# Seven block products for the attention's output product, with sums of its weights made in the first layer

## The chip, the cores and the metric

The kernel runs on one core of a Trainium2 chip. The metric is the time of one execution in microseconds (us), as the device reports it; a kernel's time is the median of several runs. In the profile PE is TensorE, DVE VectorE, ACT ScalarE, POOL GpSimd and SP SyncE, which sends all the DMAs here.

## The reference

Two layers on 1024 tokens of width 1024, all in float32. The first is a retention layer with a gated output product; the second is latent attention with eight heads of width 128. What the change touches is the end of the second layer:

```python
def mla_layer(x, g_pre, w_in, g_q_lat, w_uq, w_out, g_post, k_nope, k_rope, v):
    ...
    o = mla_attention(q_nope, q_rope, k_nope, k_rope, v)
    y = (jax.nn.silu(gate) * o) @ w_out
    return x + rmsnorm(y, g_post)
```

`w_out` is 1024 x 1024 there. The first layer ends in the same way, with a `w_out` of 2048 x 1024.

## The kernel before

Each float32 operand is kept as two parts, hi and lo, and each product of two blocks is three matmuls: hi x lo, lo x hi, hi x hi (`mm3`, L229, its matmuls on L232 to L234). `split` (L236) makes the parts: a copy on ACT (L238) and a subtraction on DVE (L239). Nearly all data lies in a heap of 51 blocks of [128, 1024] (`Heap`, L33), which are used again in the order in which they come free, so a load can wait for an old block's last reader. A framework puts the instructions of each engine into their final order, from the order of the code and its own estimate of the times; what stands in a queue is done in that order.

The program has these stages: the retention layer; its output product `out_a` (L921); norm, residual and transposes of each 128 token tile, `post_a` (L995); the latents; the gates (`gates`, L1146); the attention (`attention`, L1258). `later(n, fn)` (L259) runs a piece of work n calls of `tick` later, so beside a later product. `out_a` already works with seven block products: halves of the tokens, of the 2048 rows and of the columns. A block product has four steps b of 24 matmuls of 128x512 (`tok_product`, L822), over four PSUM banks, and two ticks for each step. Loads of `yl` (left) and `wl` (right, the sums of weights from the DRAM tiles `td`) run ahead of them. Behind the last products come the tiles' `post_a`: an ACT square, a POOL power, two DVE operations, a second square, a scaled copy `hn`, and by `later(2, transpose)` eight TensorE transposes (L1019), whose banks ACT copies into the operands of the next stage.

In the attention the scores of head h, their softmax and the products with the values go block by block (`score`, `finish`, `values`), and the projections of head h+1 are dealt out among them as filler, by a share of columns. S tiles take two banks each, two of them; `acc` and `r` have two banks each. In the last head the filler is the output product (`out_units`, L1415): for each block of 256 tokens, from the last to the first, the gated outputs `gT` are split in eight pieces of 128x256, and each half of each token tile is one bank with 24 matmuls over all eight row blocks of `w_out`:

```python
            ps = self.bank("acc")
            yield from self.project(ps, u, lambda h: [w[:, ns] for w in self.wo[h]], NH)
            nc.scalar.activation(junk[:, ns], ps, AF.Square, accum_out=ss[:, n:n + 1])
            ...
            nc.vector.tensor_mul(y[:, ns], ps, self.gpost[:, ns])
```

Then the power on POOL (L256), a DVE operation per half for scale and residual (L1448), and the stores (L1450).

Of the kernel before, what the change touches and what calls it, by code (L numbers as in the profile page):

```python
# [18 lines left out]
P = 128  # L19
# [6 lines left out]
NH = 8  # L26
# [171 lines left out]
class Trunk:  # L198
# [26 lines left out]
    def bank(self, tag, shape=(P, HALF)):  # L225
        self.n += 1
        return self.ps.tile(list(shape), F32, tag=tag, name=f"{tag}_{self.n}")
# [48 lines left out]
    def weight_order(self):  # L276

        I = self.I
        for h in range(NH):
            if h % 2 == 0:  # L280
                yield I["w_pair"][h // 2], 896
            yield I["w_head"][h], 640
        for k in range(NH):
            yield I["w_out_b"][k * P:(k + 1) * P, :], DM
# [35 lines left out]
    def run(self):  # L320
        nc, tc, ctx, I = self.nc, self.tc, self.ctx, self.I
        self.sp = ctx.enter_context(tc.tile_pool(name="sp", bufs=1))
        self.heap = Heap(ctx.enter_context(tc.tile_pool(name="mp", bufs=1)), BLOCKS)
        dp = ctx.enter_context(tc.tile_pool(name="dp", bufs=1, space=DRAM))
        self.h1 = dp.tile([NT, P, DM], F32, name="h1")
        self.td = [[dp.tile([P, DM], F32, name=f"td{n}_{b}") for b in range(4)] for n in range(4)]
        self.vd = [[dp.tile([P, DM], F32, name=f"vd{h}_{half}") for half in range(2)] for h in range(NH)]
        self.yd = [[dp.tile([P, DM], F32, name=f"yd{h}_{half}") for half in range(2)] for h in range(NH)]
        self.gd = [dp.tile([P, DM], F32, name=f"gd{h}") for h in range(NH)]
# [11 lines left out]
        with tc.tile_pool(name="psA", bufs=4, space=PSUM) as self.ps:  # L341
            self.layer_a()
            self.out_a()
            self.latents()
            self.gates()
        with tc.tile_pool(name="psB", bufs=2, space=PSUM) as self.ps:
            self.attention()
# [573 lines left out]
    def out_a(self):  # L921
# [42 lines left out]
        self.X = {}  # L964
# [3 lines left out]
        self.later(9, lambda: self.operands(("A21", "A22")))  # L968
# [5 lines left out]

        fill(0, 4)
# [14 lines left out]

    def operands(self, names):
        for n in names:
            self.operand(n, self.A[n])

    def post_a(self, g, y, gpost):  # L995

        nc, I, heap = self.nc, self.I, self.heap
        x = heap.get("xres")
        nc.sync.dma_start(x, I["x"][g * P:(g + 1) * P, :])
# [28 lines left out]
        self.later(2, transpose)  # L1028
# [117 lines left out]
    def gates(self):  # L1146
# [3 lines left out]
        away = NH - 2  # L1150
        self.gT, left = [None] * NH, [4] * NH

        def sink(p):
            def take(i, j, bank, U):
                h = 2 * p + j
                if self.gT[h] is None:
                    self.gT[h] = heap.get("gT")
                c = self.gT[h][:, i * HALF:(i + 1) * HALF]
# [5 lines left out]
                left[h] -= 2  # L1164
                if not left[h] and h < away:
                    nc.sync.dma_start(self.gd[h], self.gT[h])
                    heap.free(self.gT[h])

            return take

        def back(h):
            self.gT[h] = heap.get("gT")
            nc.sync.dma_start(self.gT[h], self.gd[h])

        for p in range(NH // 2):
            if p == NH // 2 - 1:
                for n in (2, 3):
                    self.later(n, lambda n=n: self.prefetch(n - 1))
                for h in range(away):
                    self.later(4 + h, lambda h=h: back(h))  # L1180
# [9 lines left out]
    def head_projections(self, h):  # L1190
# [4 lines left out]
        def bank():  # L1195
# [3 lines left out]
            return self.bank("S", (P, 2, HALF))[:, 0, :] if h == 0 and n % 2 else self.bank("acc")  # L1199
# [58 lines left out]
    def attention(self):  # L1258
# [15 lines left out]
        for h in range(NH):  # L1274
# [4 lines left out]
            else:  # L1279
# [3 lines left out]
                share = (own + 24 * HALF * 4) / 8  # L1283
            for step in range(8):
# [15 lines left out]
                if h == NH - 1 and 1 <= step < 5:  # L1300
                    for _ in range(2):
                        self.prefetch(1)
                        self.wo.append(self.loaded.popleft())
            if h + 1 < NH:
                for _ in fill:
                    pass
        while open_tiles:
            self.finish(open_tiles.popleft())
        self.finish(None)
# [73 lines left out]
    def values(self, h, b, pT, blocks):  # L1383
# [8 lines left out]
        u = self.gT[h][:, b * 256:(b + 1) * 256]  # L1392
# [7 lines left out]
    def prepare_out(self):  # L1400
        heap = self.heap
# [5 lines left out]
        self.out_ready = set()  # L1407
        self.gpost = heap.get("gpostb")
        self.nc.sync.dma_start(self.gpost, self.I["g_post_b"])
        self.wo = []  # L1410
        self.lead = 2
        while len(self.fetched) < 2:
            self.fetch()

    def out_units(self):  # L1415

        nc, heap = self.nc, self.heap
        for b in range(NT // 2 - 1, -1, -1):
            blocks = [[heap.get("u", F32R) for _ in range(2)] for _ in range(2)]
            part = lambda x, h: x[h // 4][:, (h % 4) * 256:(h % 4) * 256 + 256]  # L1420
            for h in range(NH):
                while h == NH - 1 and b not in self.out_ready:
                    yield 0
                self.split(part(blocks[0], h), part(blocks[1], h), self.gT[h][:, b * 256:(b + 1) * 256])
            for i in (1, 0):
                yield from self.out_tile(2 * b + i, lambda h: [part(x, h)[:, i * P:(i + 1) * P] for x in blocks])
            heap.free(*blocks[0], *blocks[1])

    def out_tile(self, t, u):
# [3 lines left out]
        y, res, junk = heap.get("yb"), heap.get("hres"), heap.get("junkb")  # L1433
        nc.sync.dma_start(res, self.h1[t])
        for n in range(2):
            ns = slice(n * HALF, (n + 1) * HALF)
            ps = self.bank("acc")
            yield from self.project(ps, u, lambda h: [w[:, ns] for w in self.wo[h]], NH)
            nc.scalar.activation(junk[:, ns], ps, AF.Square, accum_out=ss[:, n:n + 1])
# [4 lines left out]
            nc.vector.tensor_mul(y[:, ns], ps, self.gpost[:, ns])  # L1444
        heap.free(junk)
        for n in range(2):
            ns = slice(n * HALF, (n + 1) * HALF)
            nc.vector.scalar_tensor_tensor(out=y[:, ns], in0=y[:, ns], scalar=r, in1=res[:, ns],  # L1448
                                           op0=ALU.mult, op1=ALU.add)
            nc.sync.dma_start(self.out[c, ns], y[:, ns])  # L1450
        heap.free(y, res)

# [31 lines left out]
def _layout(a):  # L1484
# [37 lines left out]
    L["w_out_b"] = A["w_out_b"][0]  # L1522
# [23 lines left out]
```

## Time and profile before

| | us |
|---|---|
| median of 3 runs | 1267.18 (1267.08 to 1267.78) |
| profiled execution | 1268.73 |
| its span | 1267.0 |
| PE busy | 1240.5 (98%) |
| DVE busy | 996.6 (79%) |
| ACT busy | 639.6 (50%) |

The granted clock is 0.999 of full speed over the span. The profile shows one execution; the busy time of PE holds matmuls that overlap at their ends, so a stage is read by TensorE's gaps and by the spacing of its work, and not by the sum of durations.

### The profile page before, as it was taken

What the parts mean: (1) busy time and instruction counts of PE and PEld (TensorE: products, weight loads), DVE (VectorE), ACT (ScalarE), POOL (GpSimd) and SP (SyncE); (2) the same over time, 40 slices, a digit from 0 to 9 for tenths busy, and PEclk for the clock granted to TensorE, in tenths of its full rate; (3) what the DMA queues carried; (4) which work ended last, traced back from release to release, by engine and by line L of the source; (5) the groups of instructions that cost most, each with busy time, mean ns of one, the idle gap of its engine ahead of it and who ended that gap; (6) DMA issues with size and microseconds to landing.
All of it is one profiled execution on the core that took longest, in us unless ns stands there. A gap on an engine that the chain in (4) does not pass through costs nothing. (4 is left out here: it accounts for less than half of the span.)

```text
span 1267.0 us, 17676 instructions
## 1 busy us (share of the span) xinstructions
PE 1240.5 (98%) x6568; PEld 1066.5 (84%) x6568; DVE 996.6 (79%) x1839; ACT 639.6 (50%) x1162; POOL 65.5 (5%) x86
## 2 busy tenths in 40 slices
PE   6999999999999999999999999999999999999997
PEld 5888878888888888888888789978898989898886
DVE  6888878898998998999966874675688788989622
ACT  7632125555564565565634875574445455456411
POOL 2000000000000000001000131200000000000000
PEclk9999999999999999999999999999999999999999
DMA  8248981232222322248663631124301020122321
GB/s 349 84 154 319 325 318 50 73 112 70 86 67 85 120 67 69 84 137 338 209 245 99 234 141 34 40 96 163 118 19 51 11 57 14 34 78 100 117 84 50
DMA packets 54166, 155.32 MB, mean 123 GB/s; under 512 B 6464, under 2 KB 15680, under 8 KB 54080
## 3 DMA queue, kind: packets, MB, share of 16 engines
q1 hardware_dynamic: 54080, 154.20, 34.9%
q8 instruction: 51, 0.84, 0.3%
q14 instruction: 35, 0.29, 0.1%
HBM read 113.28 MB, written 36.70 MB: 118 GB/s over the span
## 5 line engine op out<-in xcount | busy, mean ns | idle before, releaser
L232 PE MATMUL acc<-xhi,unit 128*128 128x512 f32 x560 | 220.6, 394 | 1.4 <-DVE unit L239 1.2
L233 PE MATMUL acc<-xlo,unit 128*128 128x512 f32 x560 | 219.2, 392 | 0.8 <-DVE xlo L239 0.8
L234 PE MATMUL acc<-xhi,unit 128*128 128x512 f32 x560 | 218.2, 390 | 0.0
L232 PEld LDWEIGHTS acc<-xhi,unit 128*128 128x128 f32 x560 | 105.3, 188 | 23.1 <-DVE unit L239 2.8
L234 PEld LDWEIGHTS acc<-xhi,unit 128*128 128x128 f32 x560 | 105.2, 188 | 21.7
L233 PEld LDWEIGHTS acc<-xlo,unit 128*128 128x128 f32 x560 | 105.4, 188 | 20.4 <-DVE xlo L239 1.1
L232 PE MATMUL acc<-vhi,xlo 128*128 128x512 f32 x224 | 89.3, 399 | 1.0 <-DVE xlo L239 1.0
L234 PE MATMUL acc<-vhi,xhi 128*128 128x512 f32 x224 | 88.4, 394 | 0.0
L233 PE MATMUL acc<-vlo,xhi 128*128 128x512 f32 x224 | 88.3, 394 | 0.0
L238 ACT ACTIVATE unit<-wsum 128x512 fp32r<-128x512 f32 x80 | 50.4, 631 | 59.9 <-PE acc L234 44.9
L1346 ACT ACTIVATE p<-S,nm 128x896 f32<-128x896 f32 (+3 forms) x64 | 47.4, 741 | 54.9 <-DVE nm L1343 50.2
L238 ACT ACTIVATE unit<-wraw 128x512 fp32r<-128x512 f32 x60 | 37.8, 630 | 53.6 <-issue 21.9
L238 ACT ACTIVATE pT<-r 128x512 fp32r<-128x512 f32 (+2 forms) x96 | 44.5, 489 | 37.8 <-PE r L1376 37.7
L238 ACT ACTIVATE vhi<-wv 128x1024 fp32r<-128x1024 f32 x28 | 29.3, 1060 | 64.4 <-PE acc L233 15.5
L239 DVE TENSOR_TENSOR unit<-wsum,unit 128x512 fp32r<-128x512 f32 x80 | 54.3, 684 | 8.5 <-ACT unit L238 8.2
L239 DVE TENSOR_TENSOR pT<-r,pT 128x512 fp32r<-128x512 f32 (+2 forms) x96 | 50.8, 549 | 4.8 <-ACT pT L238 4.5
L783 POOL TENSOR_TENSOR rg<-rg,mhalf 128x2 f32<-128x2 f32 x32 | 24.6, 769 | 548.2 <-DVE rg L782 528.0
L232 PEld LDWEIGHTS acc<-vhi,xlo 128*128 128x128 f32 x224 | 42.7, 191 | 10.1 <-DVE xlo L239 1.4
L232 PE MATMUL acc<-thi,slo 128*128 128x512 f32 x128 | 49.9, 393 | 0.6 <-DVE slo L239 0.6
L234 PEld LDWEIGHTS acc<-vhi,xhi 128*128 128x128 f32 x224 | 42.8, 191 | 9.1
L233 PEld LDWEIGHTS acc<-vlo,xhi 128*128 128x128 f32 x224 | 42.8, 191 | 8.7
L232 PE MATMUL acc<-whi,u 128*128 128x512 f32 x128 | 50.0, 391 | 0.0
(291 smaller groups left out, 3429.3 us busy)
## 6 DMA issues: line engine op xcount, KB each, us to landing
wraw<-in_w_in_a_dram SPq DMA_DIRECT2D x32, 512.0 KB, 4.1
wv<-in_w_v_dram SPq DMA_DIRECT2D x28, 512.0 KB, 6.3
wl<-in_w_out_a_dram SPq DMA_DIRECT2D x28, 512.0 KB, 6.0
yl<-yd SPq DMA_DIRECT2D x28, 512.0 KB, 4.8
vd<-vo SPq DMA_DIRECT2D x32, 256.0 KB, 2.9
td<-wl SPq DMA_DIRECT2D x16, 512.0 KB, 3.6
vt<-vd SPq DMA_DIRECT2D x16, 512.0 KB, 3.2
yd<-yT SPq DMA_DIRECT2D x16, 512.0 KB, 4.7
```

Source lines behind the costliest of these rows:

```text
L232: mm(ps, lhs[1], rhs[0], start=first, stop=False, skip_group_check=more)
L233: mm(ps, lhs[0], rhs[1], start=False, stop=False, skip_group_check=more)
L234: mm(ps, lhs[0], rhs[0], start=False, stop=last, skip_group_check=more)
L238: self.nc.scalar.activation(hi, src, AF.Copy)
L239: self.nc.vector.tensor_sub(lo, src, hi.bitcast(F32))
L783: nc.gpsimd.tensor_tensor(out=rg, in0=rg, in1=self.mhalf[:, 0:1].to_broadcast([P, 2]), op=ALU.pow)
L1346: nc.scalar.activation(p[:, :w].rearrange("p (a b) -> p a b", a=pieces), view, AF.Exp, bias=nm, accum_out=sm)
```

## The change

The output product of the attention is now done with seven products of blocks of 512 tokens x 512 rows x 512 columns. In the order of the code: P1 = A11 B11, P7, P6 and P4 as filler under the last head, then P5, P2 and P3. Each has four token tiles of 12 matmuls of 128x512. The lefts are blocks of the gated outputs or their sums (made on DVE in `left_b`, then split), the rights are B11, B21, B22 of the weights, and four sums T1 to T4. These are made in `last_sums`, which `later` spreads beside `out_a`'s third to fifth products: loads of the eight half blocks of `w_out`, eight subtractions, eight splits, and sixteen stores of the parts to DRAM tiles `tb`, from where `load_right` takes them in the last head. P1, P7, P6, P4, P5 and P2 are drained by ACT copies or DVE adds into `c1`, `u3`, `u2` or `y`; P5's four banks stay (in two S tiles), and P3 adds to them. The norm at the end (`out_tile`) now reads `y` from SBUF.

To go with it: the gates are laid out by half and pair instead of by head (six of eight blocks go to DRAM and come back, as before); the rows of x for `post_a` are loaded earlier (`load_rows`), its transposes come three ticks later instead of two, and the operands A21 and A22 ten instead of nine; the PSUM pool of the first stages is two pools, and the first head's projections begin in a bank `acc` instead of `S`.

```diff
+        for n, fn in enumerate(self.last_sums()):
+            self.later(1 + 3 * n // 2, fn)
         X = [self.bank("acc") for _ in range(HT)]
         run(X)
...
-        self.X = {}
+        self.X, self.xres = {}, {}
+        self.load_rows(1)
         for t in range(HT):
             add(y[HT + t][:, n0], X[t], U[t])
             self.later(2 * t, lambda t=t: self.post_a(HT + t, y[HT + t], gpost))
-        self.later(9, lambda: self.operands(("A21", "A22")))
+        self.later(10, lambda: self.operands(("A21", "A22")))
...
+        self.load_rows(0)
         fill(0, 4)
...
+    def last_sums(self):
+        nc, heap = self.nc, self.heap
+        sub = nc.vector.tensor_sub
+        for m in range(2):
+            w = []
+            def load(m=m, w=w):
+                w += [heap.get("wl") for _ in range(4)]
+                for x, (j, n) in zip(w, ((0, 0), (0, 1), (1, 1), (1, 0))):
+                    nc.sync.dma_start(x, self.I["w_out_b"][j, n, m])
+            def sums(w=w):
+                sub(w[0], w[1], w[0])
+                sub(w[1], w[2], w[1])
+            def more(w=w):
+                sub(w[2], w[2], w[0])
+                sub(w[3], w[3], w[2])
+            def out(n, x, m=m, w=w):
+                hl = self.split_block(w[x], name="t")
+                for a, b in zip(self.tb[n][m], hl):
+                    nc.sync.dma_start(a, b.bitcast(F32))
+                heap.free(w[x], *hl)
...
-        self.later(2, transpose)
+        self.later(3, transpose)
...
-            return self.bank("S", (P, 2, HALF))[:, 0, :] if h == 0 and n % 2 else self.bank("acc")
+            return self.bank("S", (P, 2, HALF))[:, 0, :] if h == 0 and n % 2 == 0 else self.bank("acc")
...
-                share = (own + 24 * HALF * 4) / 8
+                share = (own + 32 * 3 * HALF) / 8
...
+    def out_units(self):
+        order = ("P1", "P7", "P6", "P4", "P5", "P2", "P3")
+        rhs = {"P1": "B11", "P7": "T3", "P6": "T2", "P4": "T4", "P5": "T1", "P2": "B21", "P3": "B22"}
...
+            for t in range(HT):
+                ps = d[t] if p == "P5" else self.bank("acc")
+                yield from self.block_product(ps, left, right, t)
+                if t > 1:
+                    operand(i + 1) and p == "P5" and operand(i + 2)
+                if p == "P1":
+                    nc.scalar.copy(c1[t], ps)
+                elif p == "P7":
+                    add(u3[t], ps, c1[t])
+                elif p == "P6":
+                    add(u3[t], ps, u3[t])
+                    add(u2[t], ps, c1[t])
+                elif p == "P4":
+                    y[HT + t] = heap.get("yb")
+                    add(y[HT + t][:, n0], ps, u3[t])
+                else:
+                    add(y[HT + t][:, n1], ps, u3[t])
+                    self.out_tile(HT + t, y[HT + t])
+                if t == 0 or t == 2 and p == "P5":
+                    self.load_right(rhs[order[i + 1 + t // 2]])
...
+        for t in range(HT):
+            ps = self.bank("acc")
+            yield from self.block_product(ps, *a, t)
+            y[t] = heap.get("yb")
+            add(y[t][:, n0], ps, c1[t])
+            yield from self.block_product(d[t], *b, t, True)
+            add(y[t][:, n1], d[t], u2[t])
+            self.out_tile(t, y[t])
```

`block_product` is four calls of `mm3`, one for each of the four row blocks of 128. `left_b` makes P7's left by two subtractions, P6's by two adds and two subtractions, P3's by two subtractions; the other lefts are blocks as they are.

How the order of the engines' work moves, at three places. First TensorE, in the sixth product of `out_a`, at the first transposes of `hn` (a name's number only tells tiles apart; x4 is four instructions). Before, two tiles' transposes stand together:

```order
L1019 MATMUL acc_6556<-ident_120,hn_6480 128x128 x4
L1019 MATMUL acc_6565<-ident_120,hn_6480 128x128 x4
L1019 MATMUL acc_6598<-ident_120,hn_6497 128x128 x4
L1019 MATMUL acc_6605<-ident_120,hn_6497 128x128 x4
L232 MATMUL r_6140<-thi_6524,slo_6521 128x512
L233 MATMUL r_6140<-tlo_6525,shi_6520 128x512
```

Now one tile's stand alone, before the next 24 matmuls:

```order
L1062 MATMUL acc_6673<-ident_136,hn_6577 128x128 x4
L1062 MATMUL acc_6682<-ident_136,hn_6577 128x128 x4
L232 MATMUL r_6189<-thi_6619,slo_6616 128x512
L233 MATMUL r_6189<-tlo_6620,shi_6615 128x512
L234 MATMUL r_6189<-thi_6619,shi_6615 128x512
```

Second TensorE at the start of the last product of `out_a`, where `thi_6768` and `thi_6837` are two of its steps b. Now its tiles `acc_6861` and `acc_6923` are begun in turn, with the fourth tile's transposes between them; before, one tile was done to its end first:

```order
L1062 MATMUL acc_6800<-ident_136,hn_6651 128x128 x4
L1062 MATMUL acc_6807<-ident_136,hn_6651 128x128 x4
L232 MATMUL acc_6861<-thi_6768,slo_6765 128x512
L233 MATMUL acc_6861<-tlo_6769,shi_6764 128x512
L234 MATMUL acc_6861<-thi_6768,shi_6764 128x512
L232 MATMUL acc_6861<-thi_6768,slo_6765 128x512
L233 MATMUL acc_6861<-tlo_6769,shi_6764 128x512
L234 MATMUL acc_6861<-thi_6768,shi_6764 128x512
L1062 MATMUL acc_6893<-ident_136,hn_6742 128x128 x4
L1062 MATMUL acc_6900<-ident_136,hn_6742 128x128 x4
L232 MATMUL acc_6923<-thi_6768,slo_6765 128x512
L232 MATMUL acc_6861<-thi_6837,slo_6834 128x512
```

Third VectorE at the end of the last head. Before, its queue between the last products with the values (L1393) holds the splits of 128x256 of the next token block and the last parts of the softmax:

```order
L239 TENSOR_TENSOR u_11993<-gT_8329,u_11991 128x256
L239 TENSOR_TENSOR u_11994<-gT_8333,u_11992 128x256
L239 TENSOR_TENSOR u_11994<-gT_8335,u_11992 128x256
L239 TENSOR_TENSOR u_11994<-gT_8299,u_11992 128x256
L1393 TENSOR_TENSOR gT_8282<-acc_11830,gT_8282 128x256
L239 TENSOR_TENSOR pT_11844<-r_11851,pT_11844 128x2x128
L239 TENSOR_TENSOR u_11994<-gT_8282,u_11992 128x256
```

Now the splits of 128x1024 for P4's left (`ulo_11948`, `ulo_11952`) stand ahead of the two adds that release P6's first bank (`acc_11863`, L1554 and L1555):

```order
L239 TENSOR_TENSOR ulo_11948<-gT_8426,uhi_11947 128x1024
L239 TENSOR_TENSOR ulo_11952<-gT_8373,uhi_11951 128x1024
L1436 TENSOR_TENSOR gT_8390<-acc_11874,gT_8390 128x256
L1554 TENSOR_TENSOR u_1204_11424<-acc_11863,u_1204_11424 128x512
L1555 TENSOR_TENSOR u_1242_11861<-acc_11863,c_1202_11422 128x512
```

Some rows further the split of a weight block of B21 (`wlo_12092`, for P2) stands ahead of the add that releases P4's first bank (`acc_11972`, L1558), with the products with the gain (L1594) and the splits of P2's left among them:

```order
L1436 TENSOR_TENSOR gT_8390<-acc_11976,gT_8390 128x256
L239 TENSOR_TENSOR wlo_12092<-wraw_12089,whi_12091 128x1024
L1558 TENSOR_TENSOR yb_11993<-acc_11972,u_1204_11424 128x512
L239 TENSOR_TENSOR ulo_12145<-gT_8424,uhi_12144 128x1024
L1594 TENSOR_TENSOR zb_12072<-yb_11993,gpostb_11420 128x512
L1558 TENSOR_TENSOR yb_12016<-acc_12003,u_1204_11424 128x512
```

So the bank's release, which before waited only for a square and a product of its own tile, now has a block's load and split of another product ahead of it.

## Rows read from the trace of the kernel before

**Rows 1.** The page: busy time, share of the span and instructions of each engine.

```profile
PE 1240.5 (98%) x6568; PEld 1066.5 (84%) x6568; DVE 996.6 (79%) x1839; ACT 639.6 (50%) x1162; POOL 65.5 (5%) x86
```

**Rows 2.** Stages: length; PE, PEld, DVE, ACT, POOL busy (count); PE clock, DMA share, GB/s.

```profile
575.00:600.00 25.00, 25.00 (x134) 21.49 (x133) 24.21 (x47) 13.17 (x20) 2.54 (x4) 1.00 0.86 336
622.00:691.00 69.00, 69.00 (x306) 57.17 (x305) 45.71 (x45) 25.25 (x25) 0.00 (x0) 1.00 0.57 197
691.00:765.00 74.00, 70.42 (x376) 60.44 (x375) 61.39 (x87) 58.39 (x106) 18.57 (x19) 1.00 0.48 168
1130.00:1160.00 30.00, 29.19 (x189) 26.08 (x187) 26.90 (x71) 18.12 (x42) 0.00 (x0) 1.00 0.25 89
1160.00:1200.00 40.00, 40.00 (x219) 33.74 (x217) 28.19 (x73) 17.53 (x50) 1.21 (x2) 1.00 0.22 79
1200.00:1260.00 60.00, 60.00 (x265) 49.46 (x264) 17.92 (x39) 9.29 (x28) 2.75 (x5) 1.00 0.22 80
```

**Rows 3.** TensorE's waits: bank, line, releaser; us in total, times, longest us.

```profile
PE r L586 <- DVE xt L575: 9.0, 2, 8.6
PE r L1019 <- ACT hn L1011: 2.2, 3, 1.3
PE S L1330 <- ACT p L1346: 1.0, 2, 0.5
PE S L232 <- DVE gT L1162: 0.9, 1, 0.9
PE acc L1019 <- ACT hn L1011: 0.7, 1, 0.7
PE acc L232 <- DVE slo L239: 0.6, 1, 0.6
```

**Rows 4.** Timeline of the tail: start us, us, engine, line, operation [idle before].

```profile
1260.12 0.60 ACT L1439 ACTIVATE junkb<-acc 128x512 f32<-128x512 f32 x1 [4.75 <-PE acc L234]
1260.91 0.68 DVE L1444 TENSOR_TENSOR yb<-acc,gpostb 128x512 f32<-128x512 f32 x1
1261.80 0.55 POOL L256 TENSOR_TENSOR rb<-rb,mhalf 128x1 f32<-128x1 f32 x1 [10.33 <-DVE rb L255]
1262.38 1.41 DVE L1448 SCALAR_TENSOR_TENSOR yb<-yb,rb,hres 128x512 f32<-128x512 f32 x2 [0.73 <-POOL rb L256]
1263.16 1.00 SPq L1450 DMA_DIRECT2D out_dram<-yb  x2
```

**Rows 5.** Groups by form, 1130 to 1267, first of three lines alike: busy us, mean ns.

```profile
L232 PE MATMUL acc<-whi,u 128*128 128x512 f32 x128 | 50.0, 391 | 0.0
```

**Rows 6.** Timeline of ScalarE: squares after two neighbouring groups of 24 matmuls.

```profile
1249.24 0.60 ACT L1439 ACTIVATE junkb<-acc 128x512 f32<-128x512 f32 x1 [4.75 <-PE acc L234]
1254.68 0.60 ACT L1439 ACTIVATE junkb<-acc 128x512 f32<-128x512 f32 x1 [4.75 <-PE acc L234]
```

**Rows 7.** Timeline of TensorE, 740 to 753: transposes that waited.

```profile
742.16 1.09 PE L1019 MATMUL r<-ident,hn 128*128 128x128 f32 x8 [0.74 <-ACT hn L1011]
751.83 1.09 PE L1019 MATMUL r<-ident,hn 128*128 128x128 f32 x8 [1.26 <-ACT hn L1011]
```

**Rows 8.** Timeline of VectorE and ScalarE, 719 to 731: operations in a dense queue.

```profile
719.44 2.47 DVE L972 TENSOR_TENSOR y<-r,u 128x512 f32<-128x512 f32 x4
726.38 4.62 DVE L239 TENSOR_TENSOR xlo<-hq,xhi 128x1024 fp32r<-128x1024 f32 x4
723.19 4.01 ACT L238 ACTIVATE xhi<-hq 128x1024 fp32r<-128x1024 f32 x4
```

**Rows 9.** Timeline of SyncE's queue and VectorE: last loads of right-hand sums, end of product 5.

```profile
633.51 0.79 SPq L860 DMA_DIRECT2D wl<-td  x2
669.56 2.73 DVE L959 TENSOR_TENSOR y<-r,y 128x512 f32<-128x512 f32 x4
```

**Rows 10.** DMA issues, 1130 to 1267: count, KB each, median us to landing.

```profile
wraw<-in_w_out_b_dram SPq DMA_DIRECT2D x4, 512.0 KB, 3.5
```

**Rows 11.** Timeline of TensorE, 1155 to 1157: a score tile that waited.

```profile
1155.95 0.44 PE L1330 MATMUL S<-kT,qT 128*128 128x384 f32 x1 [0.50 <-ACT p L1346]
```

More of the change, by code (lines that the diff above doesn't have):

```diff
@@ L989, in out_a, with load_rows @@
         heap.free(gpost)
+    def load_rows(self, half):
+        for g in range(half * HT, (half + 1) * HT):
+            self.xres[g] = self.heap.get("xres")
+            self.nc.sync.dma_start(self.xres[g], self.I["x"][g * P:(g + 1) * P, :])
+    def last_sums(self):
[18 more added lines that the diff above has]
+                heap.free(w[x], *hl)
+            yield load
+            yield sums
+            yield more
+            for n, x in enumerate((0, 2, 1, 3)):
+                yield lambda n=n, x=x, out=out: out(n, x)
     def operands(self, names):
@@ L1148, in gates @@
         units = self.gate_units
-        away = NH - 2
-        self.gT, left = [None] * NH, [4] * NH
+        away = NH // 2 - 1
+        self.gT = [[None] * (NH // 2) for _ in range(2)]
+        left = [[2] * (NH // 2) for _ in range(2)]
         def sink(p):
             def take(i, j, bank, U):
[L1155 to L1158, printed above, removed]
+                if self.gT[i][p] is None:
+                    self.gT[i][p] = heap.get("gT")
+                c = self.gT[i][p][:, j * HALF:(j + 1) * HALF]
                 if U is None:
@@ L1163, in take, with back @@
                     nc.scalar.activation(c, c, AF.Silu)
[L1164 to L1167, printed above, removed]
-            return take
-        def back(h):
-            self.gT[h] = heap.get("gT")
-            nc.sync.dma_start(self.gT[h], self.gd[h])
+                left[i][p] -= 1
+                if not left[i][p] and p < away:
+                    nc.sync.dma_start(self.gd[i][p], self.gT[i][p])
+                    heap.free(self.gT[i][p])
+            return take
+        def back(i, p):
+            self.gT[i][p] = heap.get("gT")
+            nc.sync.dma_start(self.gT[i][p], self.gd[i][p])
         for p in range(NH // 2):
@@ L1178, in gates @@
                     self.later(n, lambda n=n: self.prefetch(n - 1))
-                for h in range(away):
-                    self.later(4 + h, lambda h=h: back(h))
+                for n in range(2 * away):
+                    self.later(4 + n, lambda n=n: back(n % 2, n // 2))
             self.pair(units, sink(p), over=p == NH // 2 - 1)
@@ L1306, in attention @@
                     pass
+        self.scored = True
         while open_tiles:
             self.finish(open_tiles.popleft())
+            for _ in range(8):
+                next(fill, 0)
         self.finish(None)
@@ L1415, in out_units, with block_product @@
+    def block_product(self, ps, left, right, t, more=False):
+        for k in range(4):
+            c, e = slice((k % 2) * HALF + t * P, (k % 2) * HALF + (t + 1) * P), slice((k % 2) * HALF, (k % 2 + 1) * HALF)
+            self.mm3(ps, [x[:, c] for x in left[k // 2]], [x[:, e] for x in right[k // 2]], not more and k == 0, k == 3, more)
+            yield 3 * HALF
     def out_units(self):
         nc, heap = self.nc, self.heap
[L1418 to L1422, printed above, removed]
-                    yield 0
[L1424 to L1427, printed above, removed]
@@ L1429, in out_tile @@
-    def out_tile(self, t, u):
+        add = nc.vector.tensor_add
+        order = ("P1", "P7", "P6", "P4", "P5", "P2", "P3")
+        rhs = {"P1": "B11", "P7": "T3", "P6": "T2", "P4": "T4", "P5": "T1", "P2": "B21", "P3": "B22"}
+        tiles = lambda b: [x[:, i * HALF:(i + 1) * HALF] for x in b for i in range(2)]
+        blocks = {n: [heap.get(n) for _ in range(2)] for n in ("c1", "u3")}
+        c1, u3 = tiles(blocks["c1"]), tiles(blocks["u3"])
+        y = [None] * NT
+        n0, n1 = slice(0, HALF), slice(HALF, DM)
@@ new lines, in out_units @@
+        heap.free(*blocks["u3"])
+        while not operand(5):
+            yield 0
+        operand(6)
+        a = lefts[5], self.right.pop("B21")
+        b = lefts[6], self.right.pop("B22")
+        for t in range(HT):
[6 more added lines that the diff above has]
+            self.out_tile(t, y[t])
```

118 lines of the change are left out of this document (88 added, 30 removed).

## The prediction, made before the changed kernel was run

> **What bounds the kernel now.** I read the busy line of the page first [rows 1]: TensorE works 1240.5 of 1267.0 us, so a part of the program is worth what it takes from TensorE's queue, plus the waits that it makes or ends there. The table by stages comes second [rows 2]: between 1160 and 1260, where the output product of the attention runs, TensorE is busy 40.00 of 40.00 and 60.00 of 60.00 us at a granted clock of 1.00, and VectorE falls from 28.19 of 40 to 17.92 of 60. In that stage TensorE bounds alone and VectorE has room. At the end of the first layer's output product (691 to 765) TensorE is busy 70.42 of 74.00, with VectorE at 61.39 and ScalarE at 58.39. The list of TensorE's waits [rows 3] names what is lost: 9.0 us at the start, which the change does not touch, 2.2 + 0.7 + 0.6 for the transposes and one late split at the end of that product, 0.9 at the first projection of the attention, 1.0 for the scores. Last, the tail [rows 4]: after the last square starts, at 1260.12, come a product, a power on GpSimd, two scalings and two stores, and the span ends at 1267.0.
>
> Sums are made against the profiled execution: 1268.73 us, 1267.0 of them span. The median of the runs is 1267.18, 1.55 lower, and I carry a difference in the one over to the other.
>
> **The change part by part.**
>
> *48 products fewer.* The output product takes 8 tiles x 2 halves x 24 = 384 matmuls of 128x512, three forms of 128 each [rows 5]. Seven block products of four tiles with 12 each are 336. The rows give 391 ns for one, but neighbours overlap. The squares that follow each group of 24 start at 1249.24 and 1254.68 [rows 6]: 5.44 us for 24, or 0.227 each. 48 x 0.227 = **-10.9 us**. All of it lies on the path, since TensorE had no gap there. The Trainium skill, "TensorE: Matmul & The Clock Gate", section "Back-to-back issue gap", has 131 ns as the sustained spacing at 512 columns. By that figure the saving would be an estimated 6.3 us and the sum 4.6 us smaller. The squares measure these very instructions at this clock, so I take the row.
>
> *End of the first layer's output product.* Before, two tiles' transposes stand together, and TensorE waits 0.74 and 1.26 us for two of them [rows 7]; all waits there are 3.5 us [rows 3]. Now the x rows are loaded earlier, each tile's transposes come one unit later and alone, and the last product is interleaved over its tiles. The norm of a tile has one more unit of 12 to 24 matmuls, 2.7 to 5.4 us, to become ready. That is more than the longest wait (1.3), but ScalarE and VectorE stay nearly full, and the last three tiles now end within some 7 us of each other, so their transposes come in a cluster behind the same two engines. I leave some 2 us of waits: **-1.3**, between -3.0 (nearly all gone) and +1.0 (a new one the length of the longest).
>
> *First projection of the attention.* It waited 0.9 us for the last gate sum to leave its bank [rows 3]; now it starts in a bank of the other pool, whose last user is long done. **-0.9**, between -0.9 and 0.
>
> *The sums of the output weights.* Beside products three to five of the first layer's output product come 8 subtractions and 8 splits of 128x1024 on VectorE, 8 copies on ScalarE, 8 loads and 16 stores of 512 KB. Four such splits in a row take 4.62 us and four copies 4.01 [rows 8], which gives 16 x 1.15 = 18.5 us for VectorE and 8.0 for ScalarE. From 622 to 691 VectorE has 23.3 us free and ScalarE 43.8 [rows 2]. It fits, narrowly. The 24 transfers are 12.6 MB, and 622 to 691 already moves 197 GB/s, 13.6 MB; together 26.2 MB in 69 us, or 380 GB/s, where 575 to 600 moved 336 without a gap on TensorE [rows 2]. So transfers there come late, by up to 26.2 / 0.336 - 69 = 9 us at the end. What hides this is the lead of the loads: the last sums of the right side are sent for at 633.51 and multiplied from 669.56 on, 36 us later [rows 9]. The sums and the x rows hold some ten of the 51 heap blocks, which shortens that lead, but hardly to 9. I take 0, between 0 and +4 (a late block, by about one landing).
>
> *The last head and the output stage.* From P6 on VectorE has 12 splits and 2 subtractions of 1024 (14 x 1.15 = 16.1), 24 drains of 512 (0.62 by the row of four in 2.47 us [rows 8]: 14.8), 16 products with the gain (0.68 [rows 4]: 10.9), 16 scalings (0.71: 11.3) and some 3.5 us of small ones: about 57 us. TensorE has 240 matmuls, 54.4 us, and a value product of some 3. So VectorE, which had two thirds of the last 60 us free, is now nearly as full as TensorE, and every place where its queue is in the wrong order costs TensorE time. The order shows three. (a) Before P6 its left sums come behind the last values; up to 0.3. (b) The second tile of P6 needs a bank that two adds release, and these stand behind two splits for P4: 2 x 1.15 + 2 x 0.62 - 2.7 (the matmuls of the first tile still running) = some 1 to 2, taken as 1.6. (c) The second tile of P4 needs the bank that the add of the first one releases, and that add stands behind the split of a weight block of P2. The block's load can only start when a heap block of P6's right operand is free. Landing takes 3.5 us [rows 10], copy, split and add 1.0 + 1.15 + 0.62, together 6.3, of which the rest of P6, the first tile and the value product hide some 4: 2.4, between 1.2 and 4.5. P1's start behind the split of its own right block gives 0 to 1. Together +4.5. Old waits in that stretch go: from 1130 to 1160 TensorE lacked 0.81 of 30 us [rows 2], 0.50 of it at 1155.95 for a score tile [rows 11]. Net **+3.7**, between -0.7 (VectorE's order never matters) and +9.5 (the second rival below). I take a value nearer the low end because each queue place was priced from rows, and only three are out of order.
>
> *The tail.* After the last matmul there was a square, and beside it a product from the bank, then the power and two scalings. Now an add of 0.62 from the bank stands ahead of square and product, and VectorE, with four adds and products and two scalings for every 5.4 us, comes to the last tile a little late. The stores are as before. **+1.2**, between +0.3 and +1.6.
>
> *At nothing:* the new layout of the gates (six of eight tiles go away and come back, as before) and the lefts' copies on ScalarE, which is at 9.29 of 60 us in the end stage [rows 2].
>
> Sum: -10.9 - 1.3 - 0.9 + 0 + 3.7 + 1.2 = **-8.2**. The profiled execution would be 1260.5, the median **1259.0 us**.
>
> **The rivals.**
>
> *The covers hold (full gain).* VectorE's misplaced work falls into slack: the last stage gives -0.7 instead of +3.7 and the tail +0.5. -13.3 gives 1253.9. For it: VectorE had 42 of the last 60 us free, and matmuls may be queued with their banks free. Against it: only two banks for the accumulators under the last head, and 57 us of VectorE against 57 of TensorE.
>
> *VectorE becomes the bound at the end.* Its 57 us are rows in a dense queue. Each wait for ScalarE, GpSimd's power (0.55, with 0.73 of idle time before the scaling [rows 4]) or a load adds to it, eight times for the powers alone: 8 x 0.73 = 5.8 us. That would put 3.7 + 5.8 = +9.5 in place of +3.7 and +1.6 in the tail: -2.0 in all, 1265.2. For it: the powers are now in the middle of VectorE's other work. Against it: that other work can fill the 0.73, and the order has a product or an add between most powers and their scalings.
>
> *Slower: the sums' stores and loads starve the first layer's output product.* SyncE issues in order; a store waits for its split, a split for its subtraction and its load, and behind each of the 8 pairs of stores stand the loads of yl and wl for later block products. The transfers lag by 9 us (above), and a pair of stores that is held for a landing and a split adds 3.5 + 1.15 = 4.7. If the blocks that the sums take bring the lead of 36 us under this, TensorE waits for most of it: -8.2 + 13.7 gives 1272.7. It decides when the loads lead their use by less than some 14 us. Against it: 36 is far from 14, and the one wait for a split in this product is 0.6 us [rows 3]. The Trainium skill, "DMA: Bandwidth & Descriptors", section "Specifications", has about 358 GB/s as the memory's limit for one core; no stretch of the trace here moves more for long, and with 358 in place of 336 the lag would be an estimated 4 us, with the same conclusion.
>
> *The change does not do what it says.* The order shows 336 matmuls, so only their price can fail. At 131 ns instead of 227 the sum would be -3.6, 1263.6.
>
> **How the numbers follow.** Forecast 0.56, with an own range of 1256.5 to 1262.5; full gain 0.17; VectorE the bound 0.18; SyncE's queue 0.06; the price 0.03. About 0.2% (2.5 us) is what a measurement of this kernel can tell from no change. The third case lies on that edge and gives half of itself to "same", a little of the forecast's upper end goes there too: faster 0.84, same 0.10, slower 0.06. The range goes from the full gain, 1254.0, to the VectorE case, 1265.2, and leaves out the queue case and what lies beyond the other two.
>
> **What would show it.** 336 output matmuls at the same spacing; no wait of TensorE before the first projection; about 2 us of waits for transposes between 691 and 765; no new waits for operands of products three to five; some 4 us of new waits of TensorE in the last 100 us, on adds of P6 and P4; from the last matmul to the end of the span some 8 us instead of 7. The prediction is wrong if TensorE's waits in the last 100 us are above 9 us or below 1, or if waits for operands show between 622 and 691.

## The result: some 7 us faster, by a sum whose parts were partly wrong

The changed kernel takes 1260.19 us (median of 6 runs, 1259.15 to 1262.41), the kernel before 1267.63 on the same chip: ratio 0.9945, 95% interval 0.9932 to 0.9958; that is 7.4 us by the medians and 7.0 by the ratio. Forecast were 1259.0 and a range of 1254.0 to 1265.2. The profiled execution took 1261.71, its span 1259.9.

The profile after, first the page's busy line and the table by stages (columns as in [rows 2]; the row 722 to 728 is a piece of the row above it):

```profile
PE 1231.4 (98%) x6520; PEld 1060.3 (84%) x6520; DVE 1042.7 (83%) x1871; ACT 651.7 (52%) x1154; POOL 71.9 (6%) x86
```

```profile
600.00:691.00 91.00, 91.00 (x404) 75.30 (x404) 79.26 (x77) 46.06 (x48) 0.47 (x1) 1.00 0.84 316
691.00:765.00 74.00, 68.30 (x347) 58.32 (x346) 61.78 (x81) 54.36 (x96) 22.68 (x18) 0.95 0.49 183
722.00:728.00 6.00, 5.17 (x14) 4.23 (x15) 6.00 (x8) 6.00 (x14) 0.00 (x0) 0.50 1.03 414
1130.00:1190.00 60.00, 60.00 (x367) 54.04 (x366) 49.13 (x110) 30.73 (x63) 0.00 (x0) 1.00 0.28 96
1190.00:1255.00 65.00, 60.74 (x274) 48.84 (x272) 57.87 (x96) 23.81 (x49) 5.80 (x8) 1.00 0.58 212
```

There are 48 matmuls fewer. The end of the first layer's output product is worse than before: TensorE lacks 5.7 of 74 us (3.6 in [rows 2]), and for some 6 us its granted clock is 0.50, the lower level of 1.2 GHz. The last stage has hardly a gap, though VectorE is now busy 57.87 of 65 us. The list of TensorE's waits (as in [rows 3]) and its rows on the timeline say the same:

```profile
PE acc L1062 <- ACT hq L1067: 2.8, 1, 2.8
PE r L1062 <- ACT hn L1054: 2.1, 2, 1.2
PE r L232 <- DVE slo L239: 0.7, 1, 0.7
PE acc L232 <- DVE gT L1436: 0.5, 1, 0.5
PE S L232 <- DVE yb L1560: 0.3, 1, 0.3
```

```profile
722.83 1.12 PE L1062 MATMUL acc<-ident,hn 128*128 128x128 f32 x4 [2.80 <-ACT hq L1067]
...
837.63 0.50 PE L233 MATMUL acc<-xlo,unit 128*128 128x512 f32 x1 [0.76 <-DVE xlo L239]
957.61 0.35 PE L232 MATMUL acc<-pT,v 128*128 128x256 f32 x1 [0.20 <-DVE sm L1389]
1197.65 0.50 PE L232 MATMUL acc<-thi,ulo 128*128 128x512 f32 x1 [0.47 <-DVE gT L1436]
```

Before, the same small waits at the same places end at 833.55 and 954.50, and an earlier one at 205.14 (204.52 now):

```profile
205.14 0.63 PE L693 MATMUL r<-ident,qk 128*128 128x128 f32 x4 [0.40 <-DVE qk L662]
...
833.55 0.50 PE L233 MATMUL acc<-xlo,unit 128*128 128x512 f32 x1 [0.77 <-DVE xlo L239]
...
954.50 0.35 PE L232 MATMUL acc<-pT,v 128*128 128x256 f32 x1 [0.20 <-DVE sm L1347]
...
1259.69 0.39 PE L234 MATMUL acc<-whi,u 128*128 128x512 f32 x1
```

Between these marks the traces can be laid side by side. TensorE's last matmul ends at 1259.69 + 0.39 = 1260.08 before and at 1251.16 + 0.39 = 1251.55 now.

| stretch | before | after | difference | forecast |
|---|---|---|---|---|
| start to the mark at 205 | 205.14 | 204.52 | -0.6 | 0 |
| to the mark behind the output product of the first layer | 628.41 | 633.11 | +4.7 | -1.3 |
| to the mark in the attention's first heads | 120.95 | 119.98 | -1.0 | -0.9 |
| to the last matmul | 305.58 | 293.94 | -11.6 | -7.2 |
| to the end of the span | 6.92 | 8.35 | +1.4 | +1.2 |
| span | 1267.0 | 1259.9 | -7.1 | -8.2 |

The first difference is mostly the first data of the program, for which TensorE waits 8.6 us instead of 9.0. Of the +4.7, waits make 5.62 - 3.55 = +2.1 (0.73, 2.80, 1.19 and 0.90 now), and the low clock makes most of the other 2.6: the kernel of experiment 7 below has the same first layer and the same waits there, its clock stays at 1.00, and the stretch takes 630.89 us, 2.2 less. The 2.80 us come from ScalarE's queue: the copies `hq` that empty the bank stand at 722.16 behind a scaled copy, which itself had waited for GpSimd's power, and four copies of splits, as this timeline of ScalarE shows:

```profile
717.63 1.15 ACT L1054 ACTIVATE hn<-xres,rh 128x1024 f32<-128x1024 f32 x1 [1.42 <-POOL rh L256]
718.69 1.04 ACT L238 ACTIVATE shi<-yl 128x1024 fp32r<-128x1024 f32 x1
719.64 1.04 ACT L238 ACTIVATE thi<-wl 128x1024 fp32r<-128x1024 f32 x1
720.59 0.72 ACT L238 ACTIVATE whi<-wraw 128x640 fp32r<-128x640 f32 x1
721.21 1.04 ACT L238 ACTIVATE shi<-yl 128x1024 fp32r<-128x1024 f32 x1
722.16 1.17 ACT L1067 COPY hq<-acc 128x256 f32<-128x256 f32 x4
```

So two questions were open: what in the change costs 4.7 us there, and whether VectorE is as near to the bound at the end as forecast. The first had two theories, the transposes' new place (A) and the sums of the weights (B), and within B the transfers, the engines' work and the order of SyncE's queue.

### The profile page after: what moved, and what is told of

The parts are those of the page before. It is cut to its first block, busy times and chain, and to the rows that moved or that the text cites. A ratio compares the mean times of both kernels' runs of the same rounds, so it can differ in the third digit from the quotient of the medians.

```text
span 1259.9 us, 17674 instructions
## 1 busy us (share of the span) xinstructions
PE 1231.4 (98%) x6520; PEld 1060.3 (84%) x6520; DVE 1042.7 (83%) x1871; ACT 651.7 (52%) x1154; POOL 71.9 (6%) x86
## 4 chain that ended last, share of the span: by engine, by line
PE 72%; DVE 12%; ACT 7%; issue 3%; DMA 2%; POOL 2%; SPq 1%; DVEq 0%; POOLq 0%; ACTq 0%
PE acc L232 18%; PE acc L233 18%; PE acc L234 18%; PE r L232 2%; PE r L233 2%; PE r L234 2%; PE r L1418 2%; DVE qk L665 1%; DVE xs L664 1%; ACT xs L660 1%; PE S L1372 1%; ACT xs L659 1%; PE S L1376 1%; PE S L1373 1%; PE S L1377 1%
## 5 line engine op out<-in xcount | busy, mean ns | idle before, releaser
L238 ACT ACTIVATE thi<-wl 128x1024 fp32r<-128x1024 f32 x36 | 37.8, 1057 | 26.1 <-PE r L234 11.5
L233 PE MATMUL acc<-tlo,shi 128*128 128x512 f32 x128 | 50.8, 398 | 0.0
L234 PE MATMUL acc<-thi,shi 128*128 128x512 f32 x128 | 50.7, 396 | 0.0
```

The costliest lines, as they stand in the source:

```text
L233: mm(ps, lhs[0], rhs[1], start=False, stop=False, skip_group_check=more)
L234: mm(ps, lhs[0], rhs[0], start=False, stop=last, skip_group_check=more)
L238: self.nc.scalar.activation(hi, src, AF.Copy)
```

## The experiments

Ratios are to the kernel before on the same chip; the change itself had 0.9945, and 0.9937 when it ran again.

**1. The transposes two ticks after the norm again.**

```diff
-        self.later(3, transpose)
+        self.later(2, transpose)
-        self.later(10, lambda: self.operands(("A21", "A22")))
+        self.later(9, lambda: self.operands(("A21", "A22")))
```

> The change with its transposes two ticks after the norm again instead of three, and the operands nine instead of ten. Theory A: the 2.80 us wait of the fourth tile's transposes for a bank, and the fall of the clock to 0.50 behind it (some 2.6 us), come from the tick that was added, which puts those transposes behind the start of the last product, where they take banks of the same pool. Then both go, TensorE's waits between 690 and 770 return to about 3.5 us, and the time is 1255 to 1257. Theory B: the sums of the output weights (their blocks of the heap, their copies and transfers) make operands and copies late there; then the wait stays, here or at a neighbouring row, and the time stays within 1259 to 1262.

Measured: 1261.13, 0.9939 (0.9924 to 0.9954). The wait for the bank is gone, but others take its place (waits of its TensorE):

```profile
PE r L1062 <- ACT hn L1054: 2.5, 2, 1.9
PE acc L1062 <- ACT hn L1054: 1.8, 1, 1.8
...
PE acc L232 <- ACT whi L238: 1.0, 1, 1.0
```

With 0.65 for one split that is 5.9 us between 700 and 770, against 5.6. Theory A falls: the new place only decides which row waits.

**2. The rows of x loaded in the norm's own step.**

```diff
-        self.load_rows(1)
-        self.load_rows(0)
-        x = self.xres.pop(g)
+        x = heap.get("xres")
+        nc.sync.dma_start(x, I["x"][g * P:(g + 1) * P, :])
```

> The change with the rows of x loaded in the norm's own step again, as before; everything else as changed. Theory A (the added tick): 1259 to 1262, the bank wait stays. Theory C: the rows hold eight heap blocks early and so delay the loads of the last product; then the wait of 2.80 us and the low clock go and the time is 1255 to 1257. If the early rows help the norms, the time is above 1262.

Measured: 1260.38, 0.9931 (0.9916 to 0.9946), the same as the change. The bank wait went, waits for `hn` of 1.82, 0.86 and 1.40 came, with the clock at 1.00. The early rows neither cost nor help by more than can be told.

**3. One of the eight sums' steps.**

```diff
-        for m in range(2):
...
+        def one():
+            w = heap.get("wl")
+            nc.sync.dma_start(w, self.I["w_out_b"][0, 0, 0])
+            hl = self.split_block(w, name="t")
+            for a, b in zip(self.tb[0][0], hl):
+                nc.sync.dma_start(a, b.bitcast(F32))
```

> The change with one load, one split and one pair of stores in the first layer in place of the eight, sums left out; the four sums' places in the last head read that one pair (so those products are not those of the reference; their number, loads and shapes are). Theory B: with 7 of 8 steps of the sums gone, the lost time in the first layer's output product goes, 4 to 5 us: 1255 to 1256.5. Theory A: 1259 to 1262, less at most the 0.7 us of the one late split.

Measured: 1255.82, 0.9899 (0.9882 to 0.9915). Theory B holds: without the sums' work in the first layer the loss there is gone. The stretch 691 to 770, first of the change, then of this kernel (columns as in [rows 2]):

```profile
691.00:770.00 79.00, 73.30 (x378) 63.32 (x377) 65.30 (x94) 58.98 (x107) 23.65 (x20) 0.96 0.46 172
```

```profile
691.00:770.00 79.00, 76.64 (x422) 67.67 (x421) 61.56 (x96) 59.37 (x112) 22.43 (x22) 1.00 0.37 138
```

TensorE lacks 2.4 us instead of 5.7, and the clock stays up. The stretch to the mark behind the output product takes 830.66 - 204.12 = 626.54 us, 6.6 less than with the change and 1.9 less than before. The sums' last store is sent at 669.21 (below); the price is paid after that.

**4. The first projection in a bank of S.**

```diff
-            return self.bank("S", (P, 2, HALF))[:, 0, :] if h == 0 and n % 2 == 0 else self.bank("acc")
+            return self.bank("S", (P, 2, HALF))[:, 0, :] if h == 0 and n % 2 else self.bank("acc")
```

> The change with the first head's projections starting in a bank of S again. If the bank is what took away the wait at the attention's entry, a wait of some 0.9 us of TensorE's first projection for a gate sum is back. Rival: the wait went because the gates' last adds come earlier now; then there is none.

Measured: one run, 1262.39. No wait of 0.15 us or more stands at the attention's entry. But the edit did not make TensorE start in S: the framework put four matmuls of the next tile, in a bank `acc`, ahead of it. Here are the first of them, the last gate sum, and the first matmul in S:

```profile
897.20 0.39 PE L232 MATMUL acc<-cqT,wlo 128*128 128x512 f32 x1
897.40 0.69 DVE L1205 TENSOR_TENSOR gT<-acc,u 128x512 f32<-128x512 f32 x1 [2.03 <-PE acc L234]
...
898.24 0.47 PE L232 MATMUL S<-cqT,wlo 128*128 128x512 f32 x1
```

The bank of S is begun just behind that sum (897.40 + 0.69 = 898.09), as before the change. In the change the first projection begins in `acc` at 897.51, while the last gate sum runs from 897.71 to 898.40, and S follows at 899.55. So a start in `acc` covers the wait in both kernels, and this run does not speak against the bank as the reason. The two pools and the new layout of the gates were not tried apart.

**5. One pair of stores instead of eight.**

```diff
-                for a, b in zip(self.tb[n][m], hl):
-                    nc.sync.dma_start(a, b.bitcast(F32))
+                if n == 0 and m == 0:
+                    for a, b in zip(self.tb[n][m], hl):
+                        nc.sync.dma_start(a, b.bitcast(F32))
```

> The change with all loads, subtractions and splits of the sums in the first layer, but of their eight pairs of stores only the first; the four sums' places in the last head read that pair (so those products are not those of the reference; number, loads and shapes are). It tells the transfers apart from the engines' work. If the 4 to 5 us that the sums cost are transfers (the DMA engines' share stands at 1.00 from 650 to 690), 7.3 of the 12.6 MB are gone, the share falls, and the time is 1255 to 1257.5. If they are VectorE's and ScalarE's time, or the heap's blocks, it is 1259 to 1262.

Measured: 1257.13, 0.9909 (0.9894 to 0.9923). Fourteen stores are some 3.5 to 4.5 us of the loss (from 0.9937 or 0.9945 to 0.9909); loads, sums and splits together can be no more than the rest, which this interval doesn't separate from nothing.

**6. The subtractions on GpSimd.**

```diff
-        sub = nc.vector.tensor_sub
+        sub = nc.gpsimd.tensor_sub
...
-                hl = self.split_block(w[x], name="t")
+                hl = heap.get("thi", F32R), heap.get("tlo", F32R)
+                nc.scalar.copy(hl[0], w[x])
+                nc.gpsimd.tensor_sub(hl[1], w[x], hl[0])
```

> The change with the eight subtractions and the eight subtractions of the splits of the sums on GpSimd in place of VectorE. If VectorE's 18.5 us beside the products are what the sums cost: 1255 to 1257. If it is the transfers: 1259 to 1262. If GpSimd is so slow, or slows VectorE so much, that stores and norms come later: above 1262.

Measured: 1271.53, 1.0027 (1.0016 to 1.0038), 10 to 11 us slower than the change by the ratios. VectorE's splits from 622 to 691, first of the change, then of this kernel, and GpSimd's own (groups by form):

```profile
L239 DVE TENSOR_TENSOR slo<-yl,shi 128x1024 fp32r<-128x1024 f32 x12 | 14.6, 1222 | 4.7 <-ACT shi L238 2.7 <-PE acc L234 1.9
```

```profile
L239 DVE TENSOR_TENSOR slo<-yl,shi 128x1024 fp32r<-128x1024 f32 x11 | 24.3, 2216 | 0.7 <-ACT shi L238 0.7
...
L1026 POOL TENSOR_TENSOR tlo<-wl,thi 128x1024 fp32r<-128x1024 f32 x8 | 23.5, 2959 | 1.6 <-ACT thi L1025 1.6
```

A split on VectorE takes 2.2 us instead of 1.2 while GpSimd works, GpSimd takes 3.0 for its own, and TensorE then waits 6.1 us for one `hn`. The Trainium skill, "Perfetto Trace Analysis", section "Optimizing Scalar/DVE Operations", has that VectorE and GpSimd share an SBUF read port, so that moving work between them may not help. This trace agrees that it does not help (2.22 us beside GpSimd's work, 1.22 without); that the port is the reason no run here shows.

**7. The product with the gain twice.**

```diff
-            nc.vector.tensor_mul(z[:, ns], y[:, ns], self.gpost[:, ns])
+            for _ in range(2):
+                nc.vector.tensor_mul(z[:, ns], y[:, ns], self.gpost[:, ns])
```

> The change with the product with the gain in the last stage done twice: 16 more products of 128x512 on VectorE, 9.6 us by 0.60 in a row, from P5 to the end. The trace of the change has VectorE busy 39.4 of 42.5 us from 1209 to 1251.5. Theory D (VectorE is within a few us of being the bound of that stretch): 3 us fit, the rest lengthens it, plus 0.6 or 1.2 in the tail: 1265.5 to 1268.5. Theory E (banks and queues leave TensorE far ahead of VectorE's need): 1260 to 1262.5.

Measured: 1269.20, 1.0008 (0.9998 to 1.0018), a little above theory D: 8 to 9 us by the ratios for 9.6 us of work. In the traces it is 8.4: from the mark in the attention's first heads to the end of the span are 1265.6 - 954.95 = 310.65 us, in the change 302.29. Waits of TensorE, and the stages from 1209 (columns as in [rows 2]):

```profile
PE S L232 <- DVE yb L1577: 4.1, 1, 4.1
...
PE S L233 <- DVE wlo L239: 1.8, 2, 1.4
```

```profile
1209.00:1251.00 42.00, 37.11 (x160) 29.27 (x158) 40.29 (x69) 13.61 (x31) 5.50 (x6) 0.99 0.47 163
1251.00:1258.00 7.00, 5.32 (x12) 3.80 (x12) 6.74 (x13) 1.45 (x4) 0.55 (x1) 0.56 0.33 125
```

VectorE fills 40.29 of 42 us, TensorE waits, and behind the wait of 4.1 us the clock is 0.56. That clock is not the price: TensorE's last matmul ends at 1257.56, and VectorE has its backlog done only at 1257.46. In the last stage VectorE has about 1 us to give.

**8. The scalings held back by one add.**

```diff
             add(y[t][:, n0], ps, c1[t])
+            if t:
+                self.scale_out(*held)
             yield from self.block_product(d[t], *b, t, True)
             add(y[t][:, n1], d[t], u2[t])
-            self.out_tile(t, y[t])
+            held = self.out_tile(t, y[t], True)
+        self.scale_out(*held)
```

> The change with the two scalings of a tile in the last loop written after the first add of the next tile. In the change's tail VectorE waits 0.73 us for GpSimd's power and then does both scalings of the third tile, before the fourth tile's first add, whose bank was full 2.6 us earlier. If that order is the tail's 1.4 us, from the last matmul to the end of the span it is now 7.0 to 7.8 us instead of 8.35; if the add itself, between bank and square, is the tail, it stays at 8.2 to 8.5.

Measured: 1260.06 (one run). From the last matmul's end (1249.69 + 0.39) to the end of the span (1258.3) are 8.2 us. The first add moved ahead of one scaling only; the other still stands before the second add (VectorE's rows of the change, then of this kernel):

```profile
1250.13 1.41 DVE L1598 SCALAR_TENSOR_TENSOR zb<-zb,rb,hres 128x512 f32<-128x512 f32 x2 [0.73 <-POOL rb L256]
...
1251.46 0.69 DVE L1575 TENSOR_TENSOR yb<-acc,c 128x512 f32<-128x512 f32 x1
...
1252.79 0.68 DVE L1577 TENSOR_TENSOR yb<-S,u 128x512 f32<-128x512 f32 x1
```

```profile
1249.30 0.68 DVE L1575 TENSOR_TENSOR yb<-acc,c 128x512 f32<-128x512 f32 x1
...
1251.16 0.69 DVE L1579 TENSOR_TENSOR yb<-S,u 128x512 f32<-128x512 f32 x1
```

The last add starts 1.08 us after the last matmul instead of 1.24. The order of these rows is the tail's backlog, but this edit moves little of it.

**9. The stores from GpSimd's queue.**

```diff
-                    nc.sync.dma_start(a, b.bitcast(F32))
+                    nc.gpsimd.dma_start(a, b.bitcast(F32))
```

> The change with the sixteen stores of the sums sent from GpSimd's queue in place of SyncE's. Number and bytes of the transfers stay. The stores cost about 3 us by the experiment that left fourteen out. Theory F (order: loads stand behind stores that wait for VectorE in SyncE's queue): SyncE sends its loads earlier, and the time is 1256 to 1258. Theory G (bytes: the DMA engines are full from 640 to 690): 1259 to 1262. If sending from GpSimd takes VectorE's time: above 1262.

Measured: 1267.43, 0.9995 (0.9985 to 1.0004). TensorE waits 8.3 us for one `hn`. VectorE's splits keep 1.22 us, so sending from GpSimd does not slow them. SyncE is free of the stores, and the last of the right-hand sums is sent for at 652.84 instead of 659.42. But the rows of x for the first norms come later, the last at 699.18 (all four from 676.86 on in the change). Two of SyncE's waits from 655 to 700 say for what:

```profile
SPq L1082 <- DMA tb<-tlo: 7.0, 1, 7.0
SPq L1001 <- DMA tb<-thi: 5.1, 1, 5.1
```

Loads of the latents' weights (L1082) and of x (L1001) wait here until a store of the sums has landed, whose heap block they use again. In the change such waits come to 0.6 us in that stretch. Neither theory had this; how much of the loss it is, beside the new order of the queues, was not taken apart.

**10. The stores two ticks after their split, in SyncE's queue.**

```diff
-                for a, b in zip(self.tb[n][m], hl):
-                    nc.sync.dma_start(a, b.bitcast(F32))
-                heap.free(w[x], *hl)
+                heap.free(w[x])
+                def store():
+                    for a, b in zip(self.tb[n][m], hl):
+                        nc.sync.dma_start(a, b.bitcast(F32))
+                    heap.free(*hl)
+                self.later(2, store)
```

> The change with each pair of stores two ticks (one step of 24 matmuls) after its split, still in SyncE's queue, so that the parts are ready when SyncE comes to them; two heap blocks more are held meanwhile. Theory F (order): 1256 to 1258.5. Theory G (bytes): 1259 to 1262, since the same bytes go in the same stretch.

Measured: 1257.61, 0.9913 (0.9899 to 0.9928). Same bytes, same work, same engines, and most of what the stores cost is back: their place in the order decides, not their bytes. SyncE's waits at the sums' stores from 610 to 700, for the hi and the lo parts, first in the change, then here:

```profile
SPq L1026 <- ACT thi L238: 19.9, 7, 7.2
SPq L1026 <- DVE tlo L239: 14.9, 7, 5.4
```

```profile
SPq L1029 <- ACT thi L238: 10.2, 3, 5.3
...
SPq L1029 <- DVE tlo L239: 8.0, 3, 5.4
```

SyncE stands 18.2 us at these stores instead of 34.8, and TensorE's waits from 691 to 765 are 3.3 us, of 0.95, 0.94, 0.69 and 0.68, as few as before the change. What links the two is not shown. The loads that come much earlier are those of the latents' weights, by up to 10 us. What stands right ahead of such a load in the change is no store of the sums but one of `h`, which the norm makes. Rows of SyncE, first of the change, then of this kernel:

```profile
669.21 0.73 SPq L1026 DMA_DIRECT2D tb<-tlo  x1
...
712.75 0.32 SPq L1050 DMA_DIRECT2D h<-xres  x1
713.12 0.42 SPq L1082 DMA_DIRECT2D wraw<-in_w_kv_a_dram  x1
```

```profile
703.33 0.42 SPq L1087 DMA_DIRECT2D wraw<-in_w_kv_a_dram  x1
...
715.78 0.33 SPq L1055 DMA_DIRECT2D h<-xres  x1
```

Here that store of `h` comes behind the load. So the edit also moved rows that it does not name, and which of them carries the gain was not tried by itself.

**11 and 12. Both edits of 8 and 10, beside the change again.**

> The change with the stores two ticks later and the scalings held, both together. If the two edits act on different stretches, they add: the 2.6 us of the stores and the 0.2 us of the scalings, 1257.0 to 1258.0, and 2 to 3 us under the change run beside it. If the clock or the order elsewhere answers to either, it is 1258.5 or more.

> The change itself beside the kernel before it, for the comparison with the kernel above on one chip: 1259.5 to 1261.5, ratio 0.994 to 0.995. The dip of the clock behind the 2.80 us wait is in its trace again if it follows from the wait.

Measured: 1257.68, 0.9914 (0.9900 to 0.9927), beside 1261.36, 0.9937 (0.9924 to 0.9951). The two edits together give what the stores give alone. The kernels 10 and 11 beat the kernel before by 10 to 11 us, and 11 beats the change beside it by 3.7.

## Why the prediction came out right

*48 products fewer, -10.9: right.* The last stage has 336 matmuls at the same 2.72 us for 12 (a tile of P2 starts at 1245.95, its P3 at 1248.67). The Trainium skill, "TensorE: Matmul & The Clock Gate", section "Back-to-back issue gap", has 131 ns at 512 columns, by which the saving would have been an estimated 6.3 us; this trace, with 227 ns, does not agree, and the rows were the better price.

*End of the first layer's output product, -1.3, and the sums at nothing: wrong together, +4.7.* The first term was about right: with nearly all of the sums gone (experiment 3) the stretch is 1.9 us shorter than before. The sums at nothing are the term that failed. The forecast looked for their price where they stand. There it was right: from 600 to 691 TensorE is busy 91.00 of 91.00 us. But the lead that it counted on shrank from 36 us to some 10, under the 14 of the third rival; the last load of a right-hand sum and the end of the product before it are now

```profile
659.42 0.48 SPq L863 DMA_DIRECT2D wl<-td  x1
669.00 2.73 DVE L964 TENSOR_TENSOR y<-r,y 128x512 f32<-128x512 f32 x4 [1.03 <-PE r L234]
```

and still TensorE does not wait; this load is for the last of that next product's four steps. (From 650 to 690 the transfers reach 391 GB/s, more than the 336 and the 358 that the forecast worked with.) It failed in the sentence that a late block was all that could come of it. Moved stores were counted as bytes and not as places in SyncE's order; what their place changes is the next stage, whose transposes wait for engines that were already nearly full. Experiments 3, 5 and 10 show it, up to the link that stays open there. The third rival had named the queue, but put the wait at operands of the product and at 13.7 us.

*First projection, -0.9: right.* It starts in `acc` while the last gate sum still runs, as said (rows at experiment 4).

*The last stage, +3.7: wrong, -0.8.* VectorE's load was forecast well (about 57 us from P6 on; 57.87 from 1190 to 1255), and experiment 7 shows it near the bound. What failed are the terms (b) and (c), taken as 1.6 and 2.4; the sum written for (b) gives only 0.8. Their bank was misread: the second tile of P6 and of P4 takes the bank of a value product that stands between the tiles, and the bank of the first tile goes to the third, 2.7 us later. For (b) the wait of 0.47 us at 1197.65 names its releaser, the product with the gate; for (c) the add behind the weight's split starts at 1210.62, and TensorE had begun the second tile at 1209.50 without a wait. The old waits went as forecast. A further 0.6 us lies in the spacing of matmuls, not in waits, and was not taken apart.

*The tail, +1.2: right, +1.4.* An add of 0.69 and a backlog of 1.24 us on VectorE, as described.

So two errors of +6.0 and -4.4 us nearly cancelled, beside small ones; that the total came out is in good part luck. By a sign that the prediction itself named, TensorE's waits in the last 100 us below 1 us, it was wrong there: they are 0.82 us in this trace (0.47 and 0.35), and 1.21 when the change ran again. Instead of some 2 us of waits for transposes from 691 to 765 there were 4.9, and 0.7 for a split. The case of full gain needed a clean first layer; the VectorE case needed more of its work, of which only about 1 us would still have fitted.

## What to carry to other kernels

A step that is hidden where it stands can still be paid for in the next stage: follow what its DMAs are queued ahead of, not only their bytes, and try a later place for a store whose data is not there yet (here two ticks gave back 3 to 4 us). Before costing a wait for a bank, list who used each bank last in order of allocation; small products in between shift the turn. To learn how near an engine is to the bound, double one of its operations and see how much of the added time the kernel takes over.

## What was not expected of the hardware

GpSimd's subtractions of 128x1024 take 3.0 us and nearly double VectorE's beside them, from 1.22 to 2.22 us.

The clock fell behind TensorE's wait at 722 in some executions and not in others. The same wait of 2.76 to 2.82 us stands in five traces (the change twice, experiments 4, 7 and 8); the granted clock from 720 to 732 is 0.72, 0.86, 0.72, 1.00 and 0.86. While it is low, matmuls of 128x512 follow each other by 0.425 us instead of 0.227 (four from 724.60 to 726.30). That is worth some 2.2 us of one execution (experiment 7, with 1.00, against the change), and may be a part of why the change's runs lie 3 us apart; those of the kernel before, without such a wait, lie as far apart beside experiment 11 (1267.29 to 1270.32). What decides it stays open.
